# A gated encoder layer on one core: first x columns by halves, eight raw blocks held in SBUF, transposes and their copies in another order

## The chip, the cores and the metric

One core of a Trainium2 chip runs one encoder layer, in one launch. The metric is the device time of an execution in microseconds (us), as the median of three runs. Five engines work from queues of their own, each in its own order: PE (matmul; PEld is its weight load), DVE (vector), ACT (scalar, activation), POOL and SP. SP issues nearly all DMAs here, POOL some.

## The reference

Batch 1, 1024 tokens, width 2048, all in float32. With c the conditioning vector:

```python
mod = jax.nn.silu(c) @ w_ada + b_ada
shift, scale, gate = jnp.split(mod, 3, axis=-1)
h = rmsnorm(x, pre_g) * (1.0 + scale[:, None]) + shift[:, None]
proj = h @ w_in
q, k, v, gate_a, u, gate_p = jnp.split(proj, SPLIT_POINTS, axis=-1)
y_a = windowed_gqa(q, k, v, rel_table, sink) * jax.nn.silu(gate_a)
y_p = multiscale_pool(u, w_pool_grp, pool_scale) * jax.nn.silu(gate_p)
g_a, g_p = jnp.split(jax.nn.sigmoid(h @ w_merge + b_merge), N_BRANCHES, axis=-1)
merged = g_a * (y_a @ w_br_attn) + g_p * (y_p @ w_br_pool)
return x + gate[:, None] * rmsnorm(merged @ w_out, post_g)
```

What matters here is the start: PE needs h turned (width on the partitions), and h needs x, the norm of its rows, and shift and scale, which need weights of their own.

## The kernel before, in words

All large products run as Strassen products of 2 x 2 blocks (`strassen`, line 212): seven products per pair of 128 output columns, over the moving operands B11, T3, T2, B21, T4, T1, B22 in this order, into the PSUM banks X, V and Z. Every product is made of three matmuls per slice, since each operand is split into a rounded part (hi, by ACT) and the rest (lo, by DVE). Z starts as a copy of X, which ACT makes (line 293).

Until about 82 us the kernel is in a ramp: x, the scales and the shifts still arrive, and PE does what it can. The change is all in there. The order of the ramp is written out by hand; `keep` pins an instruction to the program order of its engine, so what is called first is queued first on ACT, DVE, PE and SP.

- **The scales.** `fetch_scales` loads the weights, `row_sums` (504) makes GEMV matmuls of them with silu(c), ACT copies the sums to acc (518), two transposes PM and a reduction give columns, and `scale_columns` (522) makes of them the multiplier modc. `small_vectors` (390) turns the short vectors (b_ada, the norm gain and others) into cols, by the transpose pr.
- **x.** `fetch_row` (415) loads 128 rows by 512 columns (256 KB) of x into xt. `turn_part` (471) transposes column blocks k of the token half s into banks XT, `take_turned` (480) copies a bank to xT, on ACT or DVE. `raw_operands` (663) makes the operands of the first blocks from the banks: x times the scale, without the norm (B11 and B21 for s = 0, B12 and B22 for s = 1).
- **Plain blocks.** Blocks of the first four pairs (i = 0 to 3; "11", "21", "12", "22") are computed plainly from such operands: `plain_block` (803), matmuls PB, for j = 0 and j = 1. The weights of a pair come from wide loads (`fetch_wide`, 743) and are split by `wide_weights` (791) into whi (ACT) and wlo (DVE). `put_by` (815) copies a finished block to a tile c on ACT and stores it to ramp_d by a DMA of POOL.
- **The norm.** `square_of` (431) and `norm_row` (440) sum the squares of x's rows on ACT and DVE; `factors` (448) makes the row factors of them, `spread_factors` (454) spreads them over partitions with DVE's diag tiles and PE's matmuls RB. `sums_unshifted`, `sums_over` and `put_shifted` then make the Strassen operands with norm and shift, with the small tile dif for T3.
- **The end of the ramp.** `ramp_raws` (738) loads the weights of the next Strassen pairs (raw loads 4, 5, 6 and 7), `first_given` (831) makes the first three weights of pair 4 ahead of time. `turn_next` (848) transposes x's column blocks 4 to 7, in four rounds, and `fill_last` (725) makes B22. `run` (347) then steps through the seven products of a pair; `at` is a list of extra steps, each with the number of the product behind which it is called. ada2 and ada3 are weights for the next scales and shifts, in tiles of the pool xa (five buffers) and in slots.

SP takes its DMAs in the order scales, x and wide loads, shifts (`fetch_shifts`), raw loads 4 and 5, ada2, raw load 6, ada3.

## Time and profile before

| what | value |
|---|---|
| median of three runs | 2097.65 us (2097.09 to 2098.49) |
| the profiled execution | 2096.28 us |
| its span in the trace | 2094.5 us |
| PE busy | 2073.1 us, 99% |
| DVE busy | 1555.2 us, 74% |
| ACT busy | 1113.4 us, 53% |
| DMA, mean over the span | 228 GB/s |
| PE waiting for RB's factors, once | 1.0 us |
| PE waiting for ACT's copy of X to Z, once | 2.2 us |

A row of the timeline has the start and the length in us, the engine, the line of the kernel, the operation, what it writes <- what it reads, the shape, and how many instructions it stands for; in brackets the idle time of the engine ahead of it and what ended that. Names are those of the program. A matmul's end is modelled, so a matmul's row is longer than the distance to the next one.

### The profile page before, as it was taken

To read this page: it belongs to the slowest core of one execution; us is meant where nothing else is said; L and a number is where in the kernel's file an instruction comes from. 1 tells how busy PE (TensorE), PEld (TensorE's weight loads), DVE (VectorE), ACT (ScalarE), POOL (GpSimd) and SP (SyncE) were. 2 spreads that over 40 slices of the span, in tenths; PEclk is the share of its full clock that TensorE was granted. 3 is DMA by queue.
4 is the path that set the end of the run, shared out by engine and by line. 5 is a ranking of instruction groups with operands and counts; after the bars stand their busy time and mean duration, and the time that the engine had idled before them with its cause. 6 is when DMAs were issued, how large, how long until landed. Compare 5 with 4: busy or idle time off the path is not lost.

```text
span 2094.5 us, 29063 instructions
## 1 busy us (share of the span) xinstructions
PE 2073.1 (99%) x9526; PEld 1703.2 (81%) x9526; DVE 1555.2 (74%) x2803; ACT 1113.4 (53%) x2122; POOL 47.1 (2%) x150
## 2 busy tenths in 40 slices
PE   8999999999999999999999999999999999999998
PEld 5678888888888888888888888888888788888886
DVE  5789687777566776777777688857857977889667
ACT  5764444444574634655665443334645644768554
POOL 1100000001000000000000000010000000000000
PEclk9999999999999999999999999999999999999999
DMA  9977877887575477655554576675754566686896
GB/s 359 316 260 256 277 259 235 274 284 245 186 242 181 141 242 266 212 171 170 175 170 150 184 237 219 213 238 182 235 179 158 173 203 200 231 298 206 298 336 242
DMA packets 302881, 476.62 MB, mean 228 GB/s; under 512 B 24322, under 2 KB 139626, under 8 KB 302728
## 3 DMA queue, kind: packets, MB, share of 16 engines
q1 hardware_dynamic: 296464, 457.79, 66.6%
q0 software_dynamic: 5200, 14.85, 1.9%
q10 hardware_dynamic: 1064, 2.11, 0.3%
q8 instruction: 75, 1.23, 0.2%
q14 instruction: 78, 0.64, 0.1%
HBM read 346.70 MB, written 130.05 MB: 228 GB/s over the span
## 4 chain that ended last, share of the span: by engine, by line
PE 92%; DMA 4%; DVE 2%; ACT 1%; issue 0%; SPq 0%; DVEq 0%; ACTq 0%
PE Z L237 31%; PE V L237 20%; PE X L237 20%; PE Z L1646 2%; PE Z L1648 2%; PE Z L1647 2%; DMA ada<-in_w_ada_dram 2%; PE V L1648 1%; PE V L1646 1%; PE X L1648 1%; PE X L1646 1%; PE V L1647 1%; PE X L1647 1%; PE PT L1356 1%; PE PB L812 1%; DMA xt<-in_x_dram 1%
## 5 line engine op out<-in xcount | busy, mean ns | idle before, releaser
L96 ACT ACTIVATE whi<-raw 128x512 fp32r<-128x512 f32 (+1 forms) x528 | 314.9, 601 | 494.2 <-PE Z L237 239.0
L97 DVE TENSOR_TENSOR wlo<-raw,whi 128x512 fp32r<-128x512 f32 (+1 forms) x528 | 339.8, 649 | 148.0 <-PE Z L237 109.9
L97 DVE TENSOR_TENSOR wlo<-wr,whi 128x512 fp32r<-128x512 f32 x224 | 150.5, 688 | 50.3 <-ACT whi L96 45.6
L96 ACT ACTIVATE whi<-wr 128x512 fp32r<-128x512 f32 x224 | 138.5, 629 | 86.6 <-DVE wlo L97 32.1
L103 DVE TENSOR_TENSOR raw<-raw,raw 128x512 f32<-128x512 f32 x76 | 52.5, 690 | 93.3 <-DMA raw<-in_w_merge_dram 60.5
L237 PE MATMUL Z<-T2h,whi 128*128 128x512 f32 x328 | 89.5, 392 | 2.3 <-ACT Z L293 2.2
L96 ACT ACTIVATE whi<-ws 128x512 fp32r<-128x512 f32 (+1 forms) x88 | 53.0, 603 | 72.5 <-PE X L237 61.1
L237 PE MATMUL Z<-T2h,wlo 128*128 128x512 f32 x328 | 89.3, 391 | 1.0 <-DVE wlo L97 1.0
L237 PE MATMUL V<-T3h,whi 128*128 128x512 f32 x328 | 89.5, 392 | 0.5 <-DVE u L103 0.5
L237 PE MATMUL Z<-B22h,whi 128*128 128x512 f32 x328 | 89.9, 392 | 0.0
L237 PE MATMUL Z<-T1h,whi 128*128 128x512 f32 x328 | 89.7, 390 | 0.0
L237 PE MATMUL X<-B21h,whi 128*128 128x512 f32 x328 | 89.7, 392 | 0.0
L237 PE MATMUL X<-B11h,whi 128*128 128x512 f32 x328 | 89.5, 391 | 0.0
L237 PE MATMUL V<-T4h,whi 128*128 128x512 f32 x328 | 89.3, 391 | 0.0
L237 PE MATMUL Z<-T2l,whi 128*128 128x512 f32 x328 | 89.1, 391 | 0.0
L237 PE MATMUL X<-B11l,whi 128*128 128x512 f32 x328 | 89.1, 390 | 0.0
L237 PE MATMUL Z<-B22l,whi 128*128 128x512 f32 x328 | 88.9, 390 | 0.0
L237 PE MATMUL X<-B21l,whi 128*128 128x512 f32 x328 | 88.9, 390 | 0.0
L237 PE MATMUL Z<-T1l,whi 128*128 128x512 f32 x328 | 88.9, 389 | 0.0
L237 PE MATMUL V<-T3l,whi 128*128 128x512 f32 x328 | 88.9, 390 | 0.0
L237 PE MATMUL V<-T4h,wlo 128*128 128x512 f32 x328 | 88.9, 390 | 0.0
L237 PE MATMUL V<-T4l,whi 128*128 128x512 f32 x328 | 88.8, 390 | 0.0
(419 smaller groups left out, 4911.3 us busy)
## 6 DMA issues: line engine op xcount, KB each, us to landing
part<-part_d SPq DMA_DIRECT2D x136, 256.0 KB, 4.7
ada<-in_w_ada_dram SPq DMA_DIRECT2D x128, 256.0 KB, 5.6
raw<-in_w_merge_dram SPq DMA_DIRECT2D x64, 512.0 KB, 5.3
wr<-ws_dS SPq DMA_DIRECT2D x60, 512.0 KB, 5.3
raw<-in_w_in_dram SPq DMA_DIRECT2D x56, 512.0 KB, 4.2
wr<-in_w_out_dram SPq DMA_DIRECT2D x48, 512.0 KB, 5.1
proj_d<-part SPq DMA_DIRECT2D x68, 256.0 KB, 2.4
sw<-in_w_out_dram SPq DMA_DIRECT2D x64, 256.0 KB, 5.0
```

Source lines behind the costliest of these rows:

```text
L96: ins = (nc.scalar.activation(hi, src, AF.Copy), nc.vector.tensor_tensor(lo, src, f32(hi), ALU.subtract))
L97: nc.vector.tensor_tensor(lo, src, f32(hi), ALU.subtract))
L103: return (eng or nc.vector).tensor_tensor(o, a, b, ALU.add)
L237: nc.tensor.matmul(ps, w_[:, i], op[mov][j][m_], start=fresh and i == 0 and n == 0, stop=i == nj - 1 and n == 2, skip_group_check=True)
L812: keep(nc.tensor.matmul(opened[i, blk], w[:, kh, nt * P:(nt + 1) * P], mov[kh][m], start=j == n == 0, stop=j == 1 and n == 5, skip_group_c ...
L1356: nc.tensor.transpose(pt[:, i * P:(i + 1) * P], p[:, i * P:(i + 1) * P], ident)
L1646: nc.tensor.matmul(pb, hi, w[0], start=first, stop=False, skip_group_check=True)
L1647: nc.tensor.matmul(pb, lo, w[0], start=False, stop=False, skip_group_check=True)
L1648: nc.tensor.matmul(pb, hi, w[1], start=False, stop=last, skip_group_check=True)
```

## The change

The change touches six things.

1. `fetch_halves`: the first 512 columns of x's rows 0 to 511 are loaded in two halves of 256 columns (128 KB each), the first halves before and the second halves behind the four loads of rows 512 to 1023. The wide load of the first weights thus stands behind four half loads instead of four whole ones.
2. Transposes of column blocks 2 and 3 (both token halves, sixteen in all) no longer stand beside those of blocks 0 and 1 but behind the four plain blocks of pair 0, j = 0. Their copies to xT go with them. ACT copies the first whi ahead of B11h.
3. `scale_columns` folds an addition into b1, computed once behind cols; `small_vectors` is called one GEMV step earlier.
4. `hold` instead of `put_by` for the eight blocks of pairs 0 and 1: ACT copies them into four wide tiles of the pool xa, which keeps the five buffers full. `store_held` stores these by SP, four DMAs of 512 KB, behind the shift loads; raw loads 4 to 6, ada2 and ada3 are called behind that. The copy of block (2, "11") moves behind `factors`.
5. In `first_given` the sums of raw tiles for the third weight move ahead of dif (DVE).
6. The transposes of rounds 1 and 3 of column blocks 4 to 7 use the banks sc instead of z0 and z1 (SEEDED). Rounds 3 and 4 are copied to xT, and B22 is made, behind the products of the first Strassen pair (steps 2, 3 and 4 of `at`) instead of ahead of it; the two OPEN matmuls go.

```diff
--- before.py
+++ after.py
@@ -384,6 +384,7 @@
     nc.vector.memset(scz, 0.0)
     ones = xa2.tile([P, P], F32, name="ones")
     nc.gpsimd.memset(ones, 1.0)
+    b1 = xa2.tile([P, 4], F32, name="b1")
     shz = xa2.tile([P, 4, 32], F32, name="shz")
     nc.gpsimd.memset(shz, 0.0)
 
@@ -391,6 +392,7 @@
         pr = bank("at", "pr")
         keep(nc.tensor.transpose(pr[:, 0:104], rows, ident[0:104, 0:104]))
         keep(nc.vector.tensor_copy(cols, pr[:, 0:104]))
+        keep(nc.vector.tensor_scalar(b1, cols[:, 32:36], 1.0, None, op0=ALU.add))
 
     tab = const.tile([33, NH], F32, name="tab")
     nc.gpsimd.memset(tab, 1.0)
@@ -416,6 +418,12 @@
         for q in qs:
             xts[si, q] = slot("xt", F32)
             keep(load(xts[si, q], x[si * P:(si + 1) * P, q * 512:(q + 1) * 512]))
+
+    def fetch_halves(h):
+        for si in range(4):
+            if h == 0:
+                xts[si, 0] = slot("xt", F32)
+            keep(load(xts[si, 0][:, h * 256:(h + 1) * 256], x[si * P:(si + 1) * P, h * 256:(h + 1) * 256]))
 
     def claim_turned(ks):
         for k in ks:
@@ -444,6 +452,7 @@
         square_of(si, 1, by_vector, xts[si, 2 + by_vector])
 
     rb = xa.tile([P, 2, 512], F32, tag="xa", name="rb")
+    held = {(i, nt): xa.tile([P, 2, 512], F32, tag="xa", name=uid("held")) for i in range(2) for nt in "12"}
 
     def factors():
         t = ep.tile([P, 2, NB], F32, name="rms")
@@ -520,9 +529,10 @@
         return [partial(step, q) for q in range(kcs // 4)] + [lambda: then(sum_columns(st_["acc"], n))]
 
     def scale_columns(j, pm):
-        keep(nc.vector.tensor_tensor(modc[:, 1, :, j], pm[:, 0:2], cols[:, 32 + 2 * j:34 + 2 * j], ALU.add))
-        keep(nc.vector.scalar_tensor_tensor(modc[:, 1, :, j], modc[:, 1, :, j], 1.0,
-                                            cols[:, 48 + 2 * j:50 + 2 * j], op0=ALU.add, op1=ALU.mult))
+        for kh in range(2):
+            k = 2 * j + kh
+            keep(nc.vector.tensor_scalar(modc[:, 1, kh, j:j + 1], pm[:, kh:kh + 1], b1[:, k:k + 1],
+                                         cols[:, 48 + k:49 + k], op0=ALU.add, op1=ALU.mult))
 
     def shift_columns(pm):
         keep(nc.vector.tensor_tensor(modc[:, 0, :, 0:2], pm.rearrange("p (j h) -> p h j", h=2),
@@ -660,15 +670,13 @@
 
     right = {}
 
-    def raw_operands(j, s, turned=False, between=lambda: None):
+    def raw_operands(j, s, turned=False):
 
         for kh, name in enumerate(("B11", "B21") if s == 0 else ("B12", "B22")):
             k = 2 * j + kh
             src, a = tbanks[s, k] if turned else xT[k, s], modc[:, 1, kh, j:j + 1]
             hi, lo = right[j] if name == "B12" else op[name][j]
             keep(nc.scalar.activation(hi, src, AF.Copy, scale=a))
-            if kh == 0:
-                between()
             keep(nc.vector.scalar_tensor_tensor(lo, src, a, f32(hi), op0=ALU.mult, op1=ALU.subtract))
 
     def block_of(j, kh, s):
@@ -753,11 +761,11 @@
     keep(nc.scalar.activation(scz[:, :, 0], pc[:, 0:16], AF.Silu))
     keep(nc.scalar.activation(sc, pc[:, 0:16], AF.Silu))
     scales = [fetch_scales(0)]
-    for si in range(4):
-        fetch_row(si, (0,))
+    fetch_halves(0)
     fetch_wide(0, 0, 0, 256)
     for si in range(4, 8):
         fetch_row(si, (0,))
+    fetch_halves(1)
     fetch_wide(0, 0, 256, 512)
     claim_turned(range(4))
     for j in range(2):
@@ -779,12 +787,6 @@
     claim_turned(range(4, 8))
     for j in range(2):
         claim(j, ("T3", "T2"))
-    ramp_raws(4, (0, 1))
-    ramp_raws(5, (0, 1))
-    ada2 = [ada_tile(2, q) for q in range(4)]
-    ada2 = [at[:, kk] for at in ada2 for kk in range(2)] + ada_slots(2, range(8, KT))
-    ramp_raws(6, (0, 1))
-    ada3 = ada_slots(3)
 
     weights0 = {}
 
@@ -812,6 +814,14 @@
             keep(nc.tensor.matmul(opened[i, blk], w[:, kh, nt * P:(nt + 1) * P], mov[kh][m], start=j == n == 0,
                                   stop=j == 1 and n == 5, skip_group_check=True))
 
+    def hold(i, blk):
+        keep(nc.scalar.activation(held[i, blk[0]][:, int(blk[1]) - 1], opened.pop((i, blk)), AF.Copy))
+
+    def store_held():
+        for (i, nt), t in held.items():
+            r0 = (int(nt) - 1) * P
+            keep(store(ramp_d[i][r0:r0 + P, :], t.rearrange("p a n -> p (a n)")))
+
     def put_by(i, blk):
 
         t = ev.tile([P, 512], F32, tag="ev", name=uid("c"))
@@ -836,9 +846,6 @@
             keep(sub(src, a11, a21))
         else:
             src = a11
-        if n == 2:
-            keep(add(a21, a21, a22))
-            keep(sub(a11, a21, a11))
         hi, lo = (wp.tile([P, 2, P], F32R, tag=t, name=uid(t), bufs=4) for t in ("whi", "wlo"))
         split(hi, lo, src, True)
         given.append((hi, lo))
@@ -858,24 +865,29 @@
     g[0]()
     g[1]()
     g[2]()
+    small_vectors()
     g[3]()
-    small_vectors()
+    low00 = wide_weights(0, 0)
     g[4]()
+    low00()
     turn_part(0, (0, 1), SEEDED)
-    turn_part(0, (2, 3), ("mm", "mm"))
-    raw_operands(0, 0, True, lambda: wide_weights(0, 0)())
-    for k in (0, 2, 1, 3):
-        take_turned(0, k, k % 2 == 1)
+    raw_operands(0, 0, True)
+    for k in range(2):
+        take_turned(0, k, k == 1)
     plain_block(0, "11", 0, "sc")
     plain_block(0, "21", 0, "sc")
     turn_part(1, (0, 1), ("at", "at"))
     raw_operands(0, 1, True)
-    turn_part(1, (2, 3), SEEDED)
-    for k in range(4):
-        take_turned(1, k, k % 2 == 1)
-    wide_weights(1, 0)()
+    for k in range(2):
+        take_turned(1, k, k == 1)
     plain_block(0, "12", 0, "mm")
     plain_block(0, "22", 0, "mm")
+    turn_part(1, (2, 3), ("at", "at"))
+    turn_part(0, (2, 3), SEEDED)
+    for n in (1, 0):
+        for k in (2, 3):
+            take_turned(n, k, k == 3)
+    wide_weights(1, 0)()
     for si in range(8):
         square_of(si, 0, si % 2 == 1)
     g = row_sums(scz, scales[1], partial(scale_columns, 1), 2)
@@ -891,33 +903,40 @@
     wide_weights(1, 1)()
     norm_row(0)
     plain_block(0, "11", 1)
-    put_by(0, "11")
+    hold(0, "11")
...
     norm_row(5)
     whole_block(1, "22")
-    put_by(1, "22")
+    hold(1, "22")
+    store_held()
+    ramp_raws(4, (0, 1))
+    ramp_raws(5, (0, 1))
+    ada2 = [ada_tile(2, q) for q in range(4)]
+    ada2 = [at[:, kk] for at in ada2 for kk in range(2)] + ada_slots(2, range(8, KT))
+    ramp_raws(6, (0, 1))
+    ada3 = ada_slots(3)
     norm_row(6)
     whole_block(2, "11")
-    put_by(2, "11")
     norm_row(7)
     factors()
+    put_by(2, "11")
     low = [wide_weights(3, j) for j in range(2)]
     whole_block(2, "21")
     put_by(2, "21")
@@ -942,10 +961,12 @@
     g[4]()
     first_given(0)
     first_given(1)
-    takes = turn_next(SEEDED)
+    takes = turn_next(("sc", "sc"))
     put_shifted("B11", lambda j: block_of(j, 0, 0), shift(0))
     for take in takes:
         take()
+    keep(add(*(raws[0][kh][:, :, nt * P:(nt + 1) * P] for kh, nt in ((0, 1), (0, 1), (1, 1)))))
+    keep(sub(*(raws[0][0][:, :, nt * P:(nt + 1) * P] for nt in (0, 1, 0))))
     dif = xa2.tile([P, 2], F32, name="dif")
     keep(sub(dif, modc[:, 0, 1, 0:2], modc[:, 0, 0, 0:2]))
     put_shifted("T3", lambda j: block_of(j, 0, 1), lambda j: dif[:, j:j + 1])
@@ -958,15 +979,13 @@
     whole_block(3, "22")
     put_by(3, "22")
     first_given(2)
-    takes = turn_next(SEEDED) + turn_next(("at", "at"))
+    late_takes = [turn_next(("sc", "sc")), turn_next(("at", "at"))]
     put_shifted("B21", lambda j: block_of(j, 1, 0), shift(1))
-    for take in takes:
-        take()
-    fill_last()
     early.close()
-    for tag in SEEDED:
-        hi = op["B11"][0][0]
-        keep(nc.tensor.matmul(bank(tag, "OPEN"), hi[:, 0:P], hi, start=True, stop=True))
+
+    def take_late(n):
+        for take in late_takes[n]:
+            take()
 
     group2 = modulation(2, ada2.__getitem__, True, True)
     group3 = modulation(3, ada3.__getitem__, True, True)
@@ -1005,7 +1024,8 @@
     for n, i in enumerate(range(AHEAD_PAIRS, RAMP)):
         at = [(1, partial(second_raws, n - 2))] if n > 1 else []
         if n == 0:
-            at.append((1, lambda: ramp_raws(7, (0, 1))))
+            at.extend(((1, lambda: ramp_raws(7, (0, 1))), (2, partial(take_late, 0)), (3, fill_last),
+                       (4, partial(take_late, 1))))
         if i == RAMP - 1:
             at.append((4, partial(get_parts, SECOND[0], ev)))
         run(ramp_gen((0, 1), i, None, False, given=() if n else given), side, range(7), at)
```

How instructions move, at three places. First ACT at the start, from the first copy xT to the copy acc of the second GEMV (whi is the split of a wide load, the rows xt,ssq_x are squares). Before:

```order
L485 ACTIVATE xT_177<-XT_469 128x512
L485 ACTIVATE xT_185<-XT_479 128x512
L669 ACTIVATE B12h_203<-XT_515,modc 128x512
L669 ACTIVATE B22h_199<-XT_516,modc 128x512
L485 ACTIVATE xT_179<-XT_515 128x512
L485 ACTIVATE xT_187<-XT_529 128x512
L795 ACTIVATE whi_543<-wide_166 128x512
L438 ACTIVATE xt_158,ssq_x<-xt_158 128x512
L438 ACTIVATE xt_162,ssq_x<-xt_162 128x512
L438 ACTIVATE xt_168,ssq_x<-xt_168 128x512
L438 ACTIVATE xt_172,ssq_x<-xt_172 128x512
L518 ACTIVATE acc_586<-GEMV_569 128x256
```

and after the change:

```order
L494 ACTIVATE xT_186<-XT_414 128x512
L679 ACTIVATE B12h_212<-XT_444,modc 128x512
L679 ACTIVATE B22h_208<-XT_445,modc 128x512
L494 ACTIVATE xT_188<-XT_444 128x512
L494 ACTIVATE xT_196<-XT_474 128x512
L494 ACTIVATE xT_194<-XT_484 128x512
L797 ACTIVATE whi_498<-wide_171 128x512
L446 ACTIVATE xt_163,ssq_x<-xt_163 128x512
L446 ACTIVATE xt_167,ssq_x<-xt_167 128x512
L446 ACTIVATE xt_173,ssq_x<-xt_173 128x512
L446 ACTIVATE xt_177,ssq_x<-xt_177 128x512
L527 ACTIVATE acc_527<-GEMV_510 128x256
```

Before, the copies of column block 2 (XT_479 and XT_529) stand each beside those of block 0. After the change both (XT_474 and XT_484, which PE fills behind the plain blocks) stand behind B22h, and whi, the squares and acc stay behind them.

Second, DVE near the end of the ramp, around dif (raw tiles are weights, B11l, T3l and T2l the rests of operands). Before:

```order
L720 SCALAR_TENSOR_TENSOR B11l_208<-xT_185,modc,B11h_207 128x512
L106 TENSOR_TENSOR dif<-modc 128x2
L103 TENSOR_TENSOR raw_374<-raw_374 128x2x128
L720 SCALAR_TENSOR_TENSOR T3l_356<-xT_179,dif,T3h_355 128x512
L720 SCALAR_TENSOR_TENSOR T3l_364<-xT_187,dif,T3h_363 128x512
L720 SCALAR_TENSOR_TENSOR T2l_360<-tf_851,modc,T2h_359 128x512
L720 SCALAR_TENSOR_TENSOR T2l_368<-tf_853,modc,T2h_367 128x512
L103 TENSOR_TENSOR raw_371<-raw_371 128x2x128
L106 TENSOR_TENSOR raw_371<-raw_371 128x2x128
```

and after the change:

```order
L728 SCALAR_TENSOR_TENSOR B11l_217<-xT_194,modc,B11h_216 128x512
L103 TENSOR_TENSOR raw_668<-raw_668 128x2x128
L103 TENSOR_TENSOR raw_671<-raw_671 128x2x128
L106 TENSOR_TENSOR raw_668<-raw_668 128x2x128
L106 TENSOR_TENSOR dif<-modc 128x2
L728 SCALAR_TENSOR_TENSOR T3l_365<-xT_188,dif,T3h_364 128x512
L728 SCALAR_TENSOR_TENSOR T3l_373<-xT_196,dif,T3h_372 128x512
L728 SCALAR_TENSOR_TENSOR T2l_369<-tf_849,modc,T2h_368 128x512
L728 SCALAR_TENSOR_TENSOR T2l_377<-tf_851,modc,T2h_376 128x512
```

Two sums of one raw tile have moved from behind T2l to ahead of dif, beside the sum of the other.

Third, ACT at the first Strassen pair (Z is the copy of X, p, u and c are results, whi weights, xT copies of late banks). Before:

```order
L717 ACTIVATE B21h_211<-xT_0_189,modc 128x512
L485 ACTIVATE xT_343<-XT_1017 128x512
L485 ACTIVATE xT_347<-XT_1018 128x512
L485 ACTIVATE xT_351<-XT_1027 128x512
L485 ACTIVATE xT_1_354<-XT_1028 128x512
L717 ACTIVATE B22h_199<-xT_183,modc 128x512
L717 ACTIVATE B22h_215<-xT_1_190,modc 128x512
L293 ACTIVATE Z_1055<-X_1054 128x512
L251 ACTIVATE p_240_1070<-V_1056 128x512
L96 ACTIVATE whi_1083<-raw_371 128x256
L96 ACTIVATE whi_1097<-raw_371 128x256
L96 ACTIVATE whi_1114<-raw_371 128x256
```

and after the change:

```order
L293 ACTIVATE Z_1041<-X_1040 128x512
L251 ACTIVATE p_234_1056<-V_1042 128x512
L494 ACTIVATE xT_352<-XT_1015 128x512
L494 ACTIVATE xT_356<-XT_1016 128x512
L96 ACTIVATE whi_1075<-raw_668 128x256
L251 ACTIVATE u_236_1069<-Z_1041 128x512
L725 ACTIVATE B22h_208<-xT_192,modc 128x512
L725 ACTIVATE B22h_224<-xT_1_199,modc 128x512
L332 ACTIVATE c_1085<-X_1040 128x512
L494 ACTIVATE xT_360<-XT_1025 128x512
L494 ACTIVATE xT_1_363<-XT_1026 128x512
L96 ACTIVATE whi_1091<-raw_668 128x256
```

The copies xT and the two B22h stood ahead of Z; now they stand between Z and the weights whi of the later products.

More of the change, by code (lines that the diff above doesn't have):

```diff
@@ L893, in encoder_layer @@
     plain_block(0, "11", 1)
-    put_by(0, "11")
+    hold(0, "11")
     plain_block(0, "21", 1)
-    put_by(0, "21")
+    hold(0, "21")
     norm_row(1)
     plain_block(0, "12", 1)
-    put_by(0, "12")
+    hold(0, "12")
     wide_weights(2, 0)()
@@ L902, in encoder_layer @@
     plain_block(0, "22", 1)
-    put_by(0, "22")
+    hold(0, "22")
     plain_block(1, "11", 1)
-    put_by(1, "11")
+    hold(1, "11")
     norm_row(3)
     plain_block(1, "21", 1)
-    put_by(1, "21")
+    hold(1, "21")
     wide_weights(2, 1)()
@@ L911, in encoder_layer @@
     whole_block(1, "12")
-    put_by(1, "12")
+    hold(1, "12")
     norm_row(5)
     whole_block(1, "22")
-    put_by(1, "22")
+    hold(1, "22")
[6 more added lines that the diff above has]
+    ada3 = ada_slots(3)
     norm_row(6)
     whole_block(2, "11")
-    put_by(2, "11")
     norm_row(7)
     factors()
+    put_by(2, "11")
     low = [wide_weights(3, j) for j in range(2)]
```

## The prediction

> **What bounds the kernel now.** I read the windows by stage first: three stretches, with the busy time of PE, PEld, DVE, ACT and POOL (instruction counts in brackets), the granted clock, the DMA share and GB/s.
>
> ```profile
> 10.70:26.20 15.50, 13.44 (x94) 8.98 (x93) 9.61 (x22) 9.12 (x21) 0.00 (x0) 1.00 1.08 371
> 26.20:50.90 24.70, 24.70 (x110) 20.24 (x110) 15.42 (x41) 17.50 (x41) 4.89 (x9) 1.00 1.04 394
> 78.10:86.20 8.10, 5.30 (x15) 3.79 (x15) 4.67 (x10) 6.45 (x15) 1.11 (x2) 0.79 1.11 359
> ```
>
> In the middle stretch PE is never idle: 110 matmuls in 24.70 us, 0.225 us each, so a product of six takes 1.35. (A row shows one matmul 0.39 to 0.50 long, because neighbours overlap.) The DMA engines are full there too. In the last stretch PE idles, and its clock falls to a mean of 0.79. So only stalls of PE near the start can be saved, and what is saved there moves all later PE work by as much. Next I read the timeline of the first stage, engine by engine: ACT, then DVE, then PE.
>
> ```profile
> 13.47 0.69 ACT L669 ACTIVATE B11h<-XT,modc 128x512 fp32r<-128x512 f32 x1 [2.32 <-PE XT L477]
> 14.06 0.62 ACT L795 ACTIVATE whi<-wide 128x512 fp32r<-128x512 f32 x1
> 14.58 0.68 ACT L669 ACTIVATE B21h<-XT,modc 128x512 fp32r<-128x512 f32 x1
> 16.10 1.08 ACT L485 ACTIVATE xT<-XT 128x512 f32<-128x512 f32 x2 [0.84 <-DVE B11l L672]
> 19.53 0.69 ACT L669 ACTIVATE B12h<-XT,modc 128x512 fp32r<-128x512 f32 x1 [2.35 <-PE XT L477]
> 20.11 0.68 ACT L669 ACTIVATE B22h<-XT,modc 128x512 fp32r<-128x512 f32 x1
> 21.10 1.09 ACT L485 ACTIVATE xT<-XT 128x512 f32<-128x512 f32 x2 [0.31 <-DVE B12l L672]
> 22.07 0.63 ACT L795 ACTIVATE whi<-wide 128x512 fp32r<-128x512 f32 x1
> 22.59 0.63 ACT L438 ACTIVATE xt<-xt 128x512 f32<-128x512 f32 x1
> ...
> 25.64 0.38 ACT L518 ACTIVATE acc<-GEMV 128x256 f32<-128x256 f32 x1 [0.50 <-PE GEMV L514]
> ```
>
> ```profile
> 14.71 0.69 DVE L106 TENSOR_TENSOR wlo<-wide,whi 128x512 fp32r<-128x512 f32 x1 [2.47 <-ACT whi L795]
> 15.32 0.74 DVE L672 SCALAR_TENSOR_TENSOR B11l<-XT,modc,B11h 128x512 fp32r<-128x512 f32 x1
> 15.98 0.74 DVE L672 SCALAR_TENSOR_TENSOR B21l<-XT,modc,B21h 128x512 fp32r<-128x512 f32 x1
> ```
>
> ```profile
> 18.50 1.91 PE L477 MATMUL XT<-ident,xt 128*128 128x128 f32 x16
> 20.27 0.50 PE L812 MATMUL PB<-B12h,whi 128*128 128x512 f32 x1
> ...
> 23.62 1.93 PE L514 MATMUL GEMV<-ada,scz 128*32 128x256 f32 x32
> ```
>
> See three things: the sixteen transposes at 18.50 end just as B12h is ready, so half of them cost PE nothing; GEMV follows the last plain block at once; and ACT gets to acc, behind a weight copy and four squares, 0.50 us before GEMV is done. Then the second stall, RB waiting for the row factors, and in the DMA issues the first weight load (its last number is the time to landing).
>
> ```profile
> 52.01 1.98 PE L465 MATMUL RB<-diag,ones 128*128 128x512 f32 x4 [0.96 <-DVE diag L459]
> ```
>
> ```profile
> wide<-in_w_in_dram SPq DMA_DIRECT2D x1, 256.0 KB, 5.9
> ```
>
> ```profile
> 7.83 0.38 SPq L748 DMA_DIRECT2D wide<-in_w_in_dram  x1
> ```
>
> The third stall is at the end of the ramp, in ACT's rows, with the PE rows on both sides of it.
>
> ```profile
> 70.84 1.34 ACT L717 ACTIVATE T3h<-xT,dif 128x512 fp32r<-128x512 f32 x2 [0.21 <-issue]
> 72.08 0.58 ACT L818 ACTIVATE c<-PB 128x512 f32<-128x512 f32 x1
> 72.56 1.07 ACT L485 ACTIVATE xT<-XT 128x512 f32<-128x512 f32 x2
> 73.51 1.34 ACT L717 ACTIVATE T2h<-tf,modc 128x512 fp32r<-128x512 f32 x2
> 74.74 0.60 ACT L818 ACTIVATE c<-PB 128x512 f32<-128x512 f32 x1
> 76.59 0.42 ACT L96 ACTIVATE whi<-raw 128x256 fp32r<-128x256 f32 x1 [1.26 <-DVE raw L106]
> 76.92 1.32 ACT L717 ACTIVATE B21h<-xT,modc 128x512 fp32r<-128x512 f32 x2
> 78.14 2.03 ACT L485 ACTIVATE xT<-XT 128x512 f32<-128x512 f32 x4
> 80.05 1.34 ACT L717 ACTIVATE B22h<-xT,modc 128x512 fp32r<-128x512 f32 x2
> 81.28 0.61 ACT L293 ACTIVATE Z<-X 128x512 f32<-128x512 f32 x1
> ```
>
> ```profile
> 77.54 0.61 PE L237 MATMUL V<-T3h,wlo 128*128 128x512 f32 x2
> ...
> 86.23 0.61 PE L237 MATMUL V<-T4h,whi 128*128 128x512 f32 x2
> ```
>
> Product V could be followed at 77.54 + 2 x 0.225 = 78.0. Product T4 starts at 86.23; between them lie two products, 2.7 us of work, in 8.2 us. Lost: 5.5 us, of which (1 - 0.79) x 8.1 = 1.7 is slow clock.
>
> **First x columns by halves.** The wide load lands at 7.83 + 5.9 = 13.7 today, behind four x loads. At 371 GB/s, four loads less 128 KB each are 1.4 us, so it lands at 12.3 and the first four columns with it. Bounds: if a half load took as long as a whole one, nothing is gained; much more than 1.4 cannot be, since these bytes stay. I take 1.4, as the rows around are limited by bytes. ACT now copies whi first: 12.4 instead of 14.06. B11h comes 0.5 later (14.58 - 14.06), at 12.9, B21h 0.6 behind it. DVE's wlo, B11l and B21l run back to back behind whi, so B21l and the PE work behind it come 14.06 - 12.4 = 1.65 us earlier: transposes at 16.85, B12h at 17.9. The earlier small vectors and b1 count as nothing: whi covers them; if the transpose pr waited for its loads, up to a microsecond.
>
> **Transposes put off.** Before B12h now stand eight transposes instead of sixteen. B12h waited for the first eight anyway (19.53 - 18.50 = 1.03), so the plain blocks still start at 18.6, and the gain stays 1.65. But the other eight of this place, and the eight of the first place, now come behind the blocks. These end at 23.62 - 1.65 = 21.97; sixteen transposes take 20.27 - 18.50 = 1.77, so GEMV starts at 23.74, no earlier than today. Worse is ACT, whose queue is in order. Copies xT of these banks can start at 21.97 + 1.03 = 23.0 (first pair of banks) and 0.89 later, 23.9 (second). Behind that one: its own 0.54 (half of 1.09), whi 0.52 (22.59 - 22.07), and four squares, 25.14 - 22.59 = 2.55 (acc sat idle 0.50 before 25.64). So acc starts at 27.5 instead of 25.64, and PE, which has finished GEMV at 25.7, waits. PM and everything behind is **late by 1.86 us**. Bounds: 1.0 if the copies came as early as the first pair of banks, 2.7 if DVE's four squares were as late again; I take the row sum.
>
> **Held blocks.** Eight copies on ACT go to other tiles at the same price; POOL loses eight issues, SP gains four stores of 512 KB behind the shift loads and ahead of raw loads 4 and 5, of the ada2 tiles (which need the tiles back) and all behind them. Two MB at 394 GB/s are 5.3 us by which the last x rows land earlier. RB's stall of **1.0 us** (0.96 in its row) goes, and I notice that it would go without that: PE comes to RB at 52.0 - 1.0 + 1.86 = 52.9, when the factors have been ready since 52.0. So the freed bandwidth buys nothing here. PE runs at this point 0.9 us late. The block (2, "11") copied behind the factors: nothing, its bank is not wanted for two blocks.
>
> **Late takes.** All times here are on the trace's own scale; the 0.9 is kept apart. DVE now makes three sums of raw tiles ahead of dif. Rows:
>
> ```profile
> 70.60 0.15 DVE L106 TENSOR_TENSOR dif<-modc 128x2 f32<-128x2 f32 x1
> 70.67 0.42 DVE L103 TENSOR_TENSOR raw<-raw 128x256 f32<-128x256 f32 x1
> ```
>
> Three of 0.42, overlapped to about 0.35 each: dif and so T3h 1.05 later, at 71.9. From there ACT is never idle, by distances of the rows above: T3h 1.24, c 0.48, two xT 0.95, T2h 1.24, c 0.48, whi 0.33 (its wait of 1.26 is gone, as the sums come early), B21h 1.22. Z<-X at 77.8 instead of 81.28; PE starts Z at 78.5, **0.5 stalled**. ACT goes on: p 0.5, two xT 0.95, whi of the next product, ready at 80.2. PE has done Z at 79.85: **0.4 stalled**, then X till 81.6. ACT: u 0.5, two B22h 1.23, c 0.48, two xT 0.95, and only then the whi for T4, ready at 83.7. **2.1 stalled.** T4 at 83.75 instead of 86.23: **2.5 us** gained, no more, since the takes moved from ahead of Z to ahead of T4. Bounds: 5.5 if ACT kept up everywhere, 0.8 if the clock halves again.
>
> **Sum.** +1.86 - 1.0 - 2.5 = -1.6 us. The profiled execution took 2096.28 us, 1.78 more than its span, and lies 1.4 below the median; -1.6 makes it 2094.7 and the median 2097.65 - 1.6 = 2096.0.
>
> **A rule weighed.** The clock fell after a pause of 3.9 us between V and Z that only the two OPEN matmuls broke. The two new pauses are 2.2 us (25.7 to 27.9) and 2.1 us. The Trainium skill ("TensorE: Matmul & The Clock Gate", section "HAM oscillation — how this bites in real kernels") says that gaps over some 3.4 us have to be avoided; by it neither new pause lowers the clock, and the sum stays -1.6. The trace shows a broken pause that did, so it cannot exclude it.
>
> **Rivals.** (A) The early start survives: the order of ACT does not hold acc back, and x is early enough for RB. Then -1.65 - 1.0 - 2.5 = -5.1, 2092.5. For it: 1.65 us are there at 16.85, and only here the held stores count. Against: acc stands behind copies of banks that PE fills last. (B) The clock halves after a new pause, 1.7 us each: once 2097.7. Twice, at the PM and at T4, it is **slower**: -1.6 + 3.4 = +1.8, 2099.4. It decides if a stretch with PE at work a third of the time counts as idle; the stretch that did count holds only OPEN. (C) The held stores make the loads behind them late. The raw loads that the add at 70.67 reads landed then at:
>
> ```profile
> 57.95 5.58 DMA raw<-in_w_in_dram
> ```
>
> that is 63.5, about 7 us ahead, 5 for the first readers. The same bytes stand before them in both orders, so they should land then again. If the four stores took three times their 5.3 us, 10.6 more, the loads would be 5.6 too late: -1.6 + 5.6 = +4.0, 2101.7. Full DMA engines speak for it, their even rate against. That holding does not bring x earlier is no case of its own: the sum does not use it.
>
> **Numbers.** Forecast 0.58, A 0.12, B 0.25 (once 0.18, twice 0.07), C 0.05. The forecast's own bounds, with 0.9 us either way at PM and 1.0 at T4, are 2094.1 to 2097.9; the range reaches to A and to B twice, 2092.3 to 2099.5, and leaves out C and the edge of A. Over 0.2% (4.2 us, about what a measurement of this kernel can tell from no change) faster: A and 0.02 of the forecast, 0.14; slower: C, 0.05; within: 0.81.
>
> **What would show it.** In the new trace: whi near 12.4 and transposes near 16.9; acc near 27.5 and PM near 27.9 with ACT's squares just ahead; RB without a wait; dif behind three raw sums; T4 waiting for whi of ACT, some 2 us; no half clock in the first 90 us. Wrong if acc starts before 26, if PE waits for a DMA between 60 and 100, or if T4 follows X at once.

## The result, and the profile after

The changed kernel is slower: 2103.78 us, median of eight executions (2101.16 to 2106.22), beside 2097.37 for the kernel before in the same comparison; the ratio is 1.0032 (95% interval 1.0021 to 1.0043). Forecast were 2096.0 and a range of 2092.3 to 2099.5. Its profiled execution took 2103.02 us, with a span of 2101.2.

The start went nearly as forecast. The timeline of the changed kernel, first ACT, then PE, has the wide weights' copy at 12.25, the eight transposes of the second token half at 16.76, GEMV at 23.61, and PM behind a wait for acc:

```profile
12.25 0.63 ACT L797 ACTIVATE whi<-wide 128x512 fp32r<-128x512 f32 x1 [1.11 <-DMA wide<-in_w_in_dram]
...
24.10 0.62 ACT L797 ACTIVATE whi<-wide 128x512 fp32r<-128x512 f32 x1
24.62 0.62 ACT L446 ACTIVATE xt<-xt 128x512 f32<-128x512 f32 x1
...
27.06 0.36 ACT L527 ACTIVATE acc<-GEMV 128x256 f32<-128x256 f32 x1
```

```profile
16.76 1.04 PE L486 MATMUL XT<-ident,xt 128*128 128x128 f32 x8
...
23.61 1.93 PE L523 MATMUL GEMV<-ada,scz 128*32 128x256 f32 x32
27.48 0.44 PE L507 MATMUL PM<-ident,acc 128*128 128x128 f32 x2 [1.94 <-ACT acc L527]
...
52.27 1.88 PE L474 MATMUL RB<-diag,ones 128*128 128x512 f32 x4
```

RB has no wait in brackets any more, and PE is there 0.26 us later than before (52.01). Up to here the change costs next to nothing. The loss comes in the next stretch. Windows by stage (busy time of PE, PEld, DVE, ACT and POOL, then granted clock, DMA share, GB/s), of before and of the changed kernel:

```profile
52.00:80.00 28.00, 27.12 (x146) 19.17 (x146) 23.67 (x46) 22.07 (x41) 5.96 (x30) 1.00 1.08 378
80.00:100.00 20.00, 18.07 (x89) 12.07 (x90) 11.32 (x26) 12.29 (x26) 1.11 (x2) 0.91 0.86 277
```

```profile
52.00:80.00 28.00, 22.84 (x111) 15.97 (x111) 16.32 (x31) 13.60 (x25) 3.24 (x16) 0.88 0.86 313
80.00:100.00 20.00, 17.39 (x76) 11.11 (x75) 12.37 (x26) 14.59 (x30) 2.70 (x5) 0.91 1.03 339
```

Between 52 and 80 us PE does 111 instructions where it did 146, and ACT is idle for half of it. ACT's timeline says what it waited for: rb, the copy of the RB product, with 11.97 us of idle time that a DMA ended, the store of a held tile.

```profile
49.74 0.60 ACT L828 ACTIVATE c<-PB 128x512 f32<-128x512 f32 x1 [0.43 <-PE PB L814]
62.31 1.08 ACT L475 ACTIVATE rb<-RB 128x512 f32<-128x512 f32 x2 [11.97 <-DMA ramp_d<-held]
...
70.66 0.60 ACT L527 ACTIVATE acc<-GEMV 128x512 f32<-128x512 f32 x1
```

The four stores are issued by SP from 51.47 on and take 7.8 us to land in the median; the last one, issued at 54.3, takes 7.9 and lands at 62.2:

```profile
51.47 3.13 SPq L823 DMA_DIRECT2D ramp_d<-held  x4
```

```profile
ramp_d<-held SPq DMA_DIRECT2D x4, 512.0 KB, 7.8
```

Why a copy into rb should wait for a store out of a held tile, the built program tells: rb and the fourth held tile have the same SBUF address (175744). The pool xa has five buffers and a buffer is given out where a tile is first written, not where it is named. The four held tiles were written first, the first tile of ada2 took the fifth buffer, the next three tiles of ada2 three of the held ones, and rb, named ahead of all of them but written last, got the fourth held tile's.

Behind rb everything on ACT and DVE is late. The X product shows by how much. It starts when ACT's copy c has freed the bank (ACT's rows, then PE's):

```profile
80.91 1.34 ACT L725 ACTIVATE T3h<-xT,dif 128x512 fp32r<-128x512 f32 x2 [1.22 <-DVE dif L106]
82.16 0.57 ACT L828 ACTIVATE c<-PB 128x512 f32<-128x512 f32 x1
...
89.67 1.32 ACT L725 ACTIVATE B22h<-xT,modc 128x512 fp32r<-128x512 f32 x2
90.96 0.60 ACT L332 ACTIVATE c<-X 128x512 f32<-128x512 f32 x1
91.45 1.08 ACT L494 ACTIVATE xT<-XT 128x512 f32<-128x512 f32 x2
92.41 1.04 ACT L96 ACTIVATE whi<-raw 128x256 fp32r<-128x256 f32 x3
```

```profile
71.31 0.90 PE L507 MATMUL PM<-ident,acc 128*128 128x128 f32 x3 [5.16 <-ACT acc L527]
...
82.78 0.74 PE L237 MATMUL X<-B11h,whi 128*128 128x512 f32 x2
...
92.89 0.73 PE L237 MATMUL V<-T4h,whi 128*128 128x512 f32 x2 [1.96 <-ACT whi L96]
...
98.52 0.62 PE L237 MATMUL X<-B11h,whi 128*128 128x512 f32 x2
```

The kernel before has X here:

```profile
74.41 0.71 PE L237 MATMUL X<-B11h,whi 128*128 128x512 f32 x2
```

rb is 9.14 us later than before (53.17, its row stands below); c comes 10.08 later (82.16 against 72.08), the other 0.94 being dif behind the raw sums; before, PE itself came to X 1.75 us after that copy was done, and now it comes 0.05 after it. 9.14 + 0.94 - 1.70 = 8.4, and X is 8.37 us late (82.78 against 74.41). The next pair's X is 8.35 late. At the end of the span 6.7 are left. From the next X to the matmul that stands at 230 us in the kernel before, all profiles take 139.7 to 139.8 us; from there to the end they differ by up to 6 us without any order in it, so the 1.6 between is within their scatter.

The granted clock falls to a half twice, for 6.8 us behind the long wait and for 3.4 us behind T4's:

```profile
66.10:70.30 4.20, 0.04 (x1) 0.00 (x0) 4.20 (x8) 4.20 (x9) 1.08 (x2) 1.00 1.09 371
70.30:77.20 6.90, 5.89 (x20) 5.22 (x21) 6.52 (x14) 3.12 (x7) 0.54 (x1) 0.51 0.64 232
...
90.90:94.20 3.30, 1.34 (x7) 1.05 (x6) 2.26 (x6) 2.93 (x9) 1.11 (x2) 1.00 1.09 365
94.20:97.70 3.50, 3.50 (x13) 1.23 (x12) 2.22 (x6) 0.34 (x1) 0.00 (x0) 0.51 1.11 336
```

### The profile page after: what moved, and what is told of

It reads as the page before. It is cut to its first block, busy times and chain, and to the rows that moved or that the text cites. A ratio compares the mean times of both kernels' runs of the same rounds, so it can differ in the third digit from the quotient of the medians.

```text
span 2101.2 us, 29057 instructions
## 1 busy us (share of the span) xinstructions
PE 2074.6 (99%) x9524; PEld 1704.4 (81%) x9524; DVE 1557.0 (74%) x2804; ACT 1112.0 (53%) x2122; POOL 42.7 (2%) x142
## 3 DMA queue, kind: packets, MB, share of 16 engines
q8 instruction: 75, 1.23, 0.3%
## 4 chain that ended last, share of the span: by engine, by line
PE 93%; DMA 3%; DVE 2%; ACT 1%; issue 0%; POOL 0%; DVEq 0%; ACTq 0%; SPq 0%; POOLq 0%
PE Z L237 31%; PE X L237 20%; PE V L237 20%; PE Z L1666 2%; PE Z L1668 2%; PE Z L1667 2%; PE X L1666 1%; PE V L1666 1%; PE V L1668 1%; PE X L1668 1%; PE X L1667 1%; PE V L1667 1%; PE PT L1376 1%; PE PB L814 1%; PE PV L1387 0%; DMA xt<-in_x_dram 0%
## 5 line engine op out<-in xcount | busy, mean ns | idle before, releaser
L237 PE MATMUL X<-B11h,wlo 128*128 128x512 f32 x328 | 88.8, 390 | 0.0
```

What stands on the lines that cost most here:

```text
L237: nc.tensor.matmul(ps, w_[:, i], op[mov][j][m_], start=fresh and i == 0 and n == 0, stop=i == nj - 1 and n == 2, skip_group_check=True)
```

## The experiments

The theory: rb's wait for the held store is the loss. Rival one: the new start, or the late takes. Rival two: loads behind the stores come late. Rival three: the new wait ahead of T4 with its half clock. All ratios are to the kernel before on the same chip, with 95% intervals. The medians come from several chips, on which the kernel before took 2097.37 to 2099.07, so kernels are compared by their ratios.

| kernel | PM | RB | X | next X | RB to next X | median, us | ratio |
|---|---|---|---|---|---|---|---|
| before | 26.08 | 52.01 | 74.41 | 90.17 | 36.45 | 2097.37 to 2099.07 | 1 |
| changed | 27.48 | 52.27 | 82.78 | 98.52 | 41.13 | 2103.78 | 1.0032 (1.0021 to 1.0043) |
| e1_rb_claimed | 27.77 | 52.56 | 75.90 | 86.16 | 33.60 | 2092.22 | 0.9972 (0.9962 to 0.9983) |
| e6_start_and_late | 27.37 | 52.15 | 74.34 | 89.48 | 35.62 | 2095.95 | 0.9992 (0.9983 to 1.0002) |
| e4_start_alone | 27.46 | 53.38 | 75.84 | 91.75 | 36.66 | 2098.29 | 1.0001 (0.9992 to 1.0010) |
| e5_late_takes_alone | 26.07 | 51.32 | 73.61 | 87.21 | 35.89 | 2098.10 | 0.9997 (0.9984 to 1.0009) |
| e8_t4_weights_behind | 28.25 | 53.02 | 76.37 | 88.77 | 35.75 | 2095.53 | 0.9988 (0.9979 to 0.9997) |
| e3_held_alone | 26.31 | 51.11 | 82.22 | 99.81 | 41.87 | 2106.18 | 1.0036 (1.0022 to 1.0049) |
| e7_held_claimed | 25.90 | 50.70 | 73.76 | 90.11 | 36.00 | 2095.33 | 0.9984 (0.9975 to 0.9993) |
| e10_no_held_early | 27.52 | 52.33 | 74.57 | 85.92 | 33.59 | 2093.42 | 0.9977 (0.9968 to 0.9985) |
| e14_no_start | 26.54 | 51.34 | 73.54 | 84.93 | 33.59 | 2090.00 | 0.9967 (0.9955 to 0.9980) |

"RB to next X" is that distance with half the length of the half clock in it taken off (before: 90.17 - 52.01 - 3.41 / 2), so it shows the order of the work rather than the clock. In the changed kernel this takes off too much: the first of its half clocks cost nothing (see after_again below), and without it the figure is 44.5.

**e1_rb_claimed.** One line behind the line that names rb:

```diff
     rb = xa.tile([P, 2, 512], F32, tag="xa", name="rb")
+    nc.gpsimd.memset(rb[:, :, 0:1], 0.0)
```

> The changed kernel with one line more: GpSimd writes two columns of rb where rb is named, so that rb has a buffer of its own from the start, the four held tiles have the other four, and it is three of the tiles of ada2 that take over a held tile's buffer. Nothing else is moved. Theory (ACT's copy rb<-RB waits for the store of the last held tile, since both tiles lie in one buffer, and the half clock that follows the wait doubles it): the copy comes within 1 us of the RB product instead of 10 us, ACT has no idle time of over 2 us between 50 and 62, PM's wait of 5.16 at 71.31 goes and PM is back at 65.8 to 66.6, no half clock between 66 and 78, X comes at 74.3 to 75.2 instead of 82.78, and the time is 2094.5 to 2097.0. Rival one (the late start: acc behind the squares): X stays over 80, the time over 2101. Rival two (the loads are late because they stand behind the stores): the wait of rb goes, but the tiles of ada2 and the raws come late, and a wait on DMA takes its place; 2098 to 2101.

2092.22 us, 0.9972. The wait is gone: rb follows RB, and PM has no wait at 66.28.

```profile
53.62 0.60 ACT L476 ACTIVATE rb<-RB 128x512 f32<-128x512 f32 x1 [2.98 <-PE RB L475]
```

ACT's idle time of 2.98 us ahead of rb (under 2 was expected) ends with RB and holds nothing up. X is at 75.90, 6.9 earlier than in the changed kernel but later than expected, because the scheduler, which orders what the program leaves free, had put all sixteen transposes ahead of it. It had also put the weight copies for T4 ahead of the late takes on ACT, so T4 followed at once. That is why the time is below what was expected, and it had to be taken apart.

```profile
81.32 0.62 PE L237 MATMUL X<-B21h,wlo 128*128 128x512 f32 x2
81.78 0.62 PE L237 MATMUL V<-T4h,whi 128*128 128x512 f32 x2
```

**e6_start_and_late.** The third part undone:

```diff
-    hold(0, "11")
+    put_by(0, "11")
...
-    store_held()
```

> The changed kernel without its third part: the first eight blocks go out by put_by as before, the loads stand where they stood, and the halves, the put-off transposes and the late takes stay. Theory (the held blocks alone cost): as fast as the kernel with rb in its own buffer within 1 us, 2095 to 2097, RB perhaps with the 1 us wait that the kernel before had there. Rival one (the start or the late takes cost): over 2101.

2095.95 us. Rival one falls: without the held blocks, start and late takes together cost nothing that can be measured. T4's wait is there, the wait at RB is not:

```profile
52.15 1.88 PE L473 MATMUL RB<-diag,ones 128*128 128x512 f32 x4
```

**e4_start_alone** and **e5_late_takes_alone.** The kernel before with the first or the last part of the change; of each a line or two:

```diff
-    for si in range(4):
-        fetch_row(si, (0,))
+    fetch_halves(0)
...
-    turn_part(0, (2, 3), ("mm", "mm"))
```

> The kernel before with the halves and the put-off transposes alone. By the forecast's own sum: the first modulation sum PM 1.4 to 1.9 us later (27.5 to 28.0), X and everything behind it later by 0.3 to 0.9 us, since PE's wait at RB takes up the rest; the time 2097.6 to 2098.3. Rival one (the loss of the changed kernel is made at the start): 2101 or more.

```diff
-    takes = turn_next(SEEDED) + turn_next(("at", "at"))
+    late_takes = [turn_next(("sc", "sc")), turn_next(("at", "at"))]
```

> The kernel before with the late takes alone. By the forecast's own sum: nothing moves ahead of X at 74.4, dif comes 1 us later, T4 comes at 83.7 to 84.2 instead of 86.23 behind a wait of about 2 us; the time 2095.0 to 2095.7. Rival three (the new wait ahead of T4 brings a half clock of its own): the same T4, a half clock of 3.4 us behind it that the kernel before had ahead of it, and no more than 0.5 us to either side of the kernel before.

Neither differs from the kernel before by what can be measured. The waits of PE in the start alone have PM as forecast, but RB's wait has not gone, though RB starts only at 53.38, and X comes 1.43 us late where 0.3 to 0.9 were expected:

```profile
PE PM L506 <- ACT acc L526: 1.9, 1, 1.9
PE RB L473 <- DVE diag L467: 1.0, 1, 1.0
```

The late takes alone move T4 to 83.12 behind the wait that was foreseen, but the time, 2098.10, stays over the 2095.0 to 2095.7 expected, as rival three has it. That a half clock behind T4 is the reason, the trace does not show: the profiled execution is the fastest of the twelve (2093.52) and has none. Ten of the twelve have a lower mean clock than it, 0.996 to 0.998 against 0.999.

```profile
PE V L237 <- ACT whi L96: 2.0, 1, 2.0
```

**e8_t4_weights_behind.** e1_rb_claimed with T4's weight copies held at their place in the changed kernel:

```diff
-        product(prep(a22), "T4", bv)
+        product(prep(a22, pairs_[0] == 1), "T4", bv)
```

> The changed kernel with rb in its own buffer, as in the first experiment, but with the weight copies of T4's product kept behind the second late take, where the changed kernel has them; in the first experiment the scheduler had moved ACT's two whi copies ahead of the late takes by itself. Theory (the first experiment's 2092.2 is the removed wait and this reordering, which is no part of the change): T4 waits about 2 us for ACT again, a half clock follows in some runs, the time is 2095 to 2096.5, as the kernel without the held blocks (2095.95). Rival (the reordering is worth nothing, and the time comes from the freed buffer alone): no wait ahead of T4, or one that costs nothing, 2091.5 to 2093.

2095.53 us: the wait is back, and RB to next X grows from 33.60 to 35.75. What that costs in time this pair does not settle: by the ratios it is 0.0016, or 3.4 us, against the first run of e1_rb_claimed, and 0.0003 against the second (below). But for eight transposes more ahead of X, this is the changed kernel without its fault, and the forecast's own case.

```profile
84.70 0.73 PE L237 MATMUL V<-T4h,whi 128*128 128x512 f32 x2 [2.29 <-ACT whi L96]
```

**e3_held_alone** and **e7_held_claimed.** The kernel before with `hold` and `store_held`, without and with the memset of rb.

```diff
-    put_by(0, "11")
+    hold(0, "11")
...
+    store_held()
```

> The kernel before with the held blocks alone, as the change has them. Theory (the fault lies in this part alone): rb's copy waits for the last held store, 9 to 10 us behind the RB product, PM waits about 5 us, a half clock of 3.4 to 6.8 us follows, the time 2104 to 2107, 7 to 9 us over the kernel before. Rival (it needs the other parts: the earlier blocks, the later start): under 2100.

> The kernel before with the held blocks alone and rb in a buffer of its own. Theory: the held blocks as such cost nothing and give PE's wait of 0.96 us at RB: 2096 to 2098. Rival two (loads that stand behind the held stores come late): a DMA wait of 1 us or more on PE, DVE or ACT between 60 and 130, and 2098.5 or more.

2106.18 us alone, as expected, and 2095.33 with one line more, a little under what was expected. The two rows of rb are 10.4 us apart (in the first, the releaser that is named, GEMV, had long been done; what landed just then was the last held store, issued at 53.8 and 8.3 us on its way):

```profile
62.17 1.09 ACT L467 ACTIVATE rb<-RB 128x512 f32<-128x512 f32 x2 [12.99 <-PE GEMV L515]
```

```profile
51.75 0.60 ACT L468 ACTIVATE rb<-RB 128x512 f32<-128x512 f32 x1 [2.98 <-PE RB L467]
```

Between 60 and 130 us the longest wait of PE, DVE or ACT for a DMA in e7_held_claimed is 0.6 us (ACT's, for a raw load), so rival two falls too.

**e9_squares_later.** In e1_rb_claimed:

```diff
-    for si in range(8):
-        square_of(si, 0, si % 2 == 1)
     g = row_sums(scz, scales[1], partial(scale_columns, 1), 2)
...
     raw_operands(1, 1)
+    for si in range(8):
+        square_of(si, 0, si % 2 == 1)
```

> The first experiment's kernel with the eight squares of the first x columns issued behind the raw operands of the second pair instead of ahead of acc. Theory (acc stands behind the copies and four squares on ACT, and that is PE's 1.94 us wait): PM waits 0.5 us or less, everything behind it up to RB comes 1.4 us earlier, and if the factors keep up the time is 1.4 us under the first experiment's: 2090.5 to 2091.5. Rival (the factors are then the bound at RB, since the squares come later on both engines): PE waits up to 1.4 us at RB instead, and the time stays at 2092.

PM's wait falls to 0.53 us, so acc did stand behind the squares. The median, 2092.56 us (0.9968, 0.9956 to 0.9981), is over the 2090.5 to 2091.5 expected and does not tell it from e1_rb_claimed. In its profiled execution PE works at half speed until 19 us (the eight transposes at 12.55 take 1.91 us, in e1_rb_claimed 1.04), so PM is later there in spite of the shorter wait, and the gain in time stays open.

**e10_no_held_early.** e6_start_and_late with the weights of B21 and T4 made behind the Z copy of the first pair:

```diff
+        pre = [prep(a, True) for a in (a12, a22)] if pairs_[0] == 1 else None
...
-        product(prep(a22), "T4", bv)
+        product(pre[1] if pre else prep(a22), "T4", bv)
```

> The kernel of the second experiment (halves, put-off transposes and late takes, no held blocks) with the weight copies of the B21 and T4 products kept ahead of the late takes on ACT. Theory (the 3.3 us between the first experiment and the one with T4's weights behind belong to T4's wait and the half clock that follows it, wherever rb lies and whatever the held blocks do): no wait of over 0.5 us ahead of T4, no half clock between 80 and 100, and 2095.95 less 2 to 3.5 us, so 2092.5 to 2094. Rival (it takes the held blocks): the wait stays or the time stays over 2095.

2093.42 us, by the ratios 3.1 under the kernel without the edit, with intervals that just touch; RB to next X falls from 35.62 to 33.59. So the wait ahead of T4 is a loss of its own, without the held blocks too.

**e11_after_early.** The same lines in the changed kernel, with rb left as it was; e11_again is the same kernel, after_again the changed one.

> The changed kernel, its rb still in the last held tile's buffer, with the weight copies of the B21 and T4 products kept ahead of the late takes on ACT. Theory (two separate losses): rb's copy waits for the store as in the changed kernel, PM waits 5 us and the half clock of 6.8 us follows; T4's wait and the second half clock go; 2103.8 less 2 to 3.5, so 2100 to 2102. Rival (the order of ACT was what the buffer's fault cost): under 2097.

2104.05 us (1.0029, 1.0019 to 1.0040), where 2100 to 2102 were expected. T4's wait was gone and the next X at 94.83, 3.7 us earlier than in the changed kernel, but the profiled execution gave it back behind 230 us, partly in single waits of 1.2, 1.0 and 0.6 us. So it was run again, beside the changed kernel.

> The changed kernel once more, beside the next one on one chip: 2102.5 to 2105; PM waits 5 us, T4 2 us.

> The changed kernel with the early weight copies once more, since its first time did not follow from its trace. Theory (the wait ahead of T4 and the half clock behind it are a loss of their own): 1.5 to 3.5 us under the changed kernel run beside it. Rival (with rb's wait still there, something later takes back what T4 gives): within 1 us of it, and the trace shows that what is gained by 100 us is gone by 230 us.

2104.35 us (1.0026, 1.0016 to 1.0035) and 2101.37 us (1.0018, 1.0008 to 1.0029): 3.0 us apart by the medians, as the theory has it, but 1.7 by the ratios, with intervals that overlap. The first pair had shown next to nothing, so what T4's wait costs in time in the changed kernel stays open between nothing and 3 us; the traces have the next X 2.2 to 3.7 us earlier. This second run of the changed kernel also corrects the theory. PM's wait was 2.55 us here instead of the 5 expected, no half clock followed it, and PE waited at X instead, for the same copy c:

```profile
81.83 0.73 PE L237 MATMUL X<-B11h,whi 128*128 128x512 f32 x2 [2.05 <-ACT c L828]
```

```profile
61.36 1.09 ACT L475 ACTIVATE rb<-RB 128x512 f32<-128x512 f32 x2 [9.36 <-PE PB L814]
```

From rb to X it is 20.47 us in both runs (82.78 - 62.31, 81.83 - 61.36), and 20.48 and 20.49 in the two of e11. ACT and DVE set X, and the 6.8 us of half clock at 70.3 were hidden: the recorded theory, that the half clock doubles the loss, was wrong on this.

**e14_no_start.** The kernel before with held blocks, rb claimed, late takes and early weights, but its old start; of the edit the lines of the start, against the changed kernel:

```diff
-    fetch_halves(0)
+    for si in range(4):
+        fetch_row(si, (0,))
...
+    turn_part(0, (2, 3), ("mm", "mm"))
```

> The kernel before with held blocks, rb in a buffer of its own, late takes and early weight copies, but without the halves and the put-off transposes. Theory (the start costs PE 1.4 us of wait ahead of PM and gains less): PM's wait at 26 is 0.53 instead of 1.94, RB and everything behind come 0.5 to 1.4 us earlier than in the first experiment, 2090.8 to 2092 where that one is at 2092.2. Rival (the start's earlier work is worth what its wait costs): within 0.3 us of it.

> The first experiment's kernel once more, beside the three others on one chip: 2091.5 to 2093.5, no half clock between 60 and 100.

> The kernel without the new start once more: 2089.5 to 2091.5.

2090.00 us, a little under what was expected, and 2091.04 the second time (0.9960, 0.9947 to 0.9974); e1_again had 2093.28 (0.9985, 0.9977 to 0.9994) beside the first. RB is 1.22 us earlier than in e1_rb_claimed; the 3.3 us between the medians are more than that, and no trace shows the rest. This is the version with the lowest ratio, faster than both kernels; its interval overlaps those of e1_rb_claimed, e9, e10 and others. The list of PE's waits in it from 24 to 100 us is short:

```profile
PE PM L501 <- ACT acc L521: 0.5, 1, 0.5
PE GEMV L576 <- ACT xT L488: 0.4, 1, 0.4
PE Z L237 <- ACT Z L293: 0.2, 1, 0.2
```

## Why the prediction was wrong, step by step

**First x columns by halves: right.** whi at 12.25 (forecast 12.4), transposes at 16.76 (16.85).

**Transposes put off: right in mechanism, too large.** GEMV at 23.61 (23.74), acc behind the late copies and four squares at 27.06 (27.5), PM 1.40 late instead of 1.86. Where PE has no other wait, this is paid in full: the next X is 1.23 earlier in e14_no_start than in e1_rb_claimed.

**Held blocks: the step that failed.** "Eight copies on ACT go to other tiles at the same price", and then only the tiles of ada2 were taken to need the held tiles back. Nine tiles share five buffers, and the one that needs its buffer first is rb. Two rows of the trace of before would have priced it, the shift loads on SP, which the stores follow, and rb on ACT:

```profile
40.67 15.07 SPq L544 DMA_DIRECT2D ada<-in_w_ada_dram  x16
```

```profile
53.17 0.60 ACT L466 ACTIVATE rb<-RB 128x512 f32<-128x512 f32 x1 [0.84 <-PE RB L465]
```

The shift loads end at 55.7, or at 50.4 with the 5.3 us of freed traffic that the prediction itself worked out (51.2 in the changed kernel). Four issues take SP some 3 us (four held ones took 3.13) and a landing some 6 (5.9 for the wide load), which is an estimate of 59, where rb is wanted at 53.2; measured were 62.3. The prediction asked what the stores do to the loads behind them (rival C, which did not happen) and not who waits on ACT for a buffer to be empty, and what is queued behind that: the row scaling, acc for PM, the copies that free PE's banks.

The signs that the prediction set itself did not see this step either: acc, PM, RB without a wait, the raw sums ahead of dif and T4's 2 us all came out. Only the half clock at 70.3 went against them, and none of them was a wait of ACT between 50 and 72 us.

RB's wait, it said, would go without the held blocks, since PE comes late. The runs do not agree on that: in e4_start_alone PE is 1.4 us late at RB and still waits 0.96, in e6 and e10, with the same start and no held blocks, it does not wait. What the held blocks do is bring the last x rows earlier. Counted from PM, DVE's reduction rms comes 19.8 to 20.8 us later in the profiles with held blocks (e9, which moves the squares, apart) and 22.4 to 24.2 us later in those without, and no kernel with them waits at RB. So the term of 1.0 us came true, and the held blocks are enough for it (e7, with the old start, has no wait), where the prediction had set them aside.

**Late takes: the waits right, the gain only at full clock.** T4 waited 1.96 us for whi (forecast 2.1), Z 0.30 (0.5), and the product behind Z shows no wait (0.4). But X to next X is 15.74 us where it was 15.76. Of the 2.5 us, 1.7 were the slow clock of before, and T4's new wait was followed by a half clock of its own at 94.2. In the profile of e5_late_takes_alone, which has no half clock, X to next X is 13.60, and 2.2 us of the 2.5 are there. Net of the clock, RB to next X is 0.6 to 0.8 us shorter in e5, e6 and e8, the prediction's lower bound ("0.8 if the clock halves again").

**The sum.** -1.6 was forecast. With the fault of rb removed and T4's weights in their place (e8_t4_weights_behind) the ratio 0.9988 (0.9979 to 0.9997) is -2.5 us (-4.4 to -0.6): the rest of the sum stood, partly by errors that cancel, and the missed wait is what turned it to +6.4 (2103.78 - 2097.37). One slip besides: rival C's 2101.7 is 4.05 over the median, and does not reach the 4.2 us beyond which the prediction counted it as slower.

**The rule weighed.** By the Trainium skill ("TensorE: Matmul & The Clock Gate", section "HAM oscillation — how this bites in real kernels") gaps over some 3.4 us are to be avoided, and the prediction took it that shorter ones do not lower the clock. Here a wait of 1.96 us was followed by 3.4 us of half clock; the measurement decides, and rival B, with its 1.7 us at T4, was the better guide.

## What to carry to other kernels

When a change puts more tiles into a pool whose buffers are full, list every tile of that pool in the order of its first write, and ask of each who empties the buffer that it gets and when that lands; a tile that is named early and written late has no buffer yet. A small early write claims one. And a gain that is read off a stretch with a slow clock has to be split into work and clock, since the clock can fall again at the next wait.

## What the hardware showed

The half clock comes and goes between executions of one kernel. Waits of PE of 1.9 to 2.3 us were followed by 3.4 us of half clock in some profiled executions (T4 in the changed kernel and in e6, the first PM in e11_after_early and after_again) and not in others of the same length (the first PM in the changed kernel, T4 in e5 and e8). The windows of e11_after_early show PM's case:

```profile
25.40:27.50 2.10, 0.15 (x5) 0.07 (x2) 2.10 (x7) 2.10 (x8) 0.00 (x0) 1.00 1.03 381
27.50:31.00 3.50, 3.50 (x10) 2.83 (x11) 3.01 (x9) 2.69 (x5) 0.00 (x0) 0.51 1.06 386
```

Where the wait falls goes with it. In the clock records of each run the stretches of full and half clock begin on a grid with a step of 3.413 us: in the changed kernel they last 61.44, 6.83, 17.07 and 3.41 us, which is 18, 2, 5 and 1 steps. Laid over PE's rows (their ends are modelled), PE at full clock was idle for 1.95 us or more within one step twelve times in the 17 traces, and each time the next step was at half clock. T4's wait in the changed kernel (90.93 to 92.89) lies whole in the step that begins at 90.83; that of e5 (81.15 to 83.12) is cut by the grid at 82.03, and the clock stayed full. With less idle time in a step (up to 1.94 us, in e8) it stayed full too, but for three steps of e3 and e7 with 1.4 to 1.7 us. So this is a pattern of these traces and not a shown rule; no run moved a wait against the grid.

It goes with much of the scatter: of 97 executions of the kernel before, the ten with a mean granted clock of 0.999 took 2095.1 us on average, the 53 with 0.998 2097.8, the 27 with 0.997 2099.5. One half clock of 3.4 us takes 0.0008 off the mean, and by that costs 1.7 us where PE is the bound. Kernels without a wait of 1.9 us or more behind 30 us mostly kept the 0.999 (27 of 40 executions of e1, e10 and e14, against 10 of 97), so they may gain more than the wait; no run separates the two.

The start differs as well. In the profiles of e9 and e11_again PE worked at half speed until 19 us; PM is at 30.41 in e11_again and at 27.43 in e11_after_early, the same kernel.

Last, and of the program rather than the chip: a line that only claims a buffer changed the order of PE, ACT and DVE between 74 and 90 us. The scheduler places what is not pinned, and some 2 us on PE's way from RB to the next X hung on that (33.60 in e1_rb_claimed, 35.75 in e8_t4_weights_behind).
